# Low parts of the feed-forward weights: VectorE subtractions replaced by accumulating transfers issued from GpSimd

## The chip, the cores and the metric

The kernel runs on one core of one Trainium2 chip. The metric is the device time of one execution in microseconds, lower is better. The core has five engines that work side by side: TensorE (PE: matrix products into PSUM; PEld is its weight load), VectorE (DVE), ScalarE (ACT), GpSimd (POOL) and SyncE (SP), which here only issues transfers. Sixteen DMA engines move data between DRAM and on-chip memory (SBUF), whichever engine issued the transfer. An engine runs its instructions in the order of its queue.

## What is computed

One decoder block on 512 tokens of width 1024: a retention mixer and a short convolution run beside each other on the first normed input, are gated and merged, go through `mix_w_out`, and then a feed-forward layer of hidden width 2816 follows. The change touches only the weights from `mix_w_out` on:

```python
merged = jax.nn.sigmoid(g_a) * y_a + jax.nn.sigmoid(g_b) * y_b
x = x + gt_m[:, None, :] * (merged @ mix_w_out[l])

h = modulate(rmsnorm(x, norm_ffn_g[l]), sh_f, sc_f)
f = (jax.nn.silu(h @ ffn_w_gate[l]) * (h @ ffn_w_up[l])) @ ffn_w_down[l]
x = x + gt_f[:, None, :] * f
...
return rmsnorm(x, final_norm_g)
```

All is float32. `mix_w_out` is 1024x1024, `ffn_w_gate` and `ffn_w_up` are 1024x2816, `ffn_w_down` is 2816x1024.

## The kernel before

**Three products for one.** TensorE takes operands in float32r, a rounded form of float32. So each float32 operand is split in a high part (the value rounded to float32r) and a low part (what the rounding left), and a product is the sum of three: high by low, low by high, high by high. `mm3` (line 125) issues the three; the same order stands in `tm_gemm` (line 733).

**How a weight is split.** `split` (line 110) takes a view of a raw tile: ScalarE copies it into a tile of float32r (the high part, line 112), and VectorE subtracts that from the raw weights into a second tile (the low part, line 114). One such split covers 128x1024 elements, 512 KB, and is called a part below. High and low tiles come from the pool `wp` with four buffers each (tags "hi" and "lo"); raw tiles have three buffers. A tile is written again only when everything that read the former content of its buffer is done; the framework puts in the semaphores for this.

**Loads.** `load_raw` (line 103) issues one transfer from SyncE for a raw tile, mostly 1 MB, and keeps these loads in the order of the program.

**Feature-major products.** `proj` (line 537) loads a raw tile of 1024 rows by 256 columns, splits it in two parts of 128 columns ([128, 8, 128]: partition, k tile, column), and after each split issues 24 products of 128x128 by 128x512 into one PSUM bank (`fm_gemm`, line 530). In DRAM a row of such a part is 128 columns, 512 bytes. The feed-forward's gate and up matrices go through it under names that start with "f" ("fg" and "fu"), from the third chunk of 128 columns on: 10 calls for either matrix, so 20 calls and 40 parts. The first two chunks of either matrix are split elsewhere (in halves ahead of time for the gate, in `first_ffn`, line 829, with GpSimd subtracting for the up matrix).

**Token-major products.** `tm_gemm` (line 733) handles `mix_w_out` (name "mix", 4 parts for either half of the columns) and `ffn_w_down` (name "dn": 12 k tiles in a first round and 10 in a second, for two halves of the columns each, so 6+6+5+5 = 22 parts). A part is two k tiles by 512 columns ([128, 2, 512]); a row in DRAM is 2 KB. Again 24 products use one part. The first `early` k tiles are worked off for all four groups of tokens in turn, and then each group of tokens goes through the rest, so that the parts of the rest are held until the end of the half. For "mix", `early` is 4 in the first half and 0 in the second.

**Order.** The calls follow each other in the program: mix, then norm 2 by token tiles (`norm2`, whose `rest` trails behind the products of the second half of mix), then six pairs of chunks of gate and up with the down product of their twelve chunks, then five pairs with theirs, and the last norm. In that stretch GpSimd has only the two subtractions of `first_ffn`.

The line numbers of the profile are often those of the helper that records an operation (line 62 or 64), so groups are told apart by their tiles: `w_fg_l` is the low part of a gate weight, `w_fu_h` the high part of an up weight, `w_mix` and `w_dn` those of the two token-major matrices.

Of the kernel before, what the change touches and what calls it, by code (L numbers as in the profile page):

```python
# [19 lines left out]
P = 128  # L20
S = 512
# [26 lines left out]


class InTurn:  # L50
    """an engine that, while it is strict, keeps to the order of the program"""

    def __init__(self, tc, engine):
        self.tc, self.engine, self.strict, self.last = tc, engine, False, None
# [16 lines left out]
def block_kernel(ctx, tc, x, c, positions, ada_w, ada_b, norm_mix_g, w_in, conv_w, ret_w_out,  # L71
# [38 lines left out]
    def split(view, shape, name, eng=None):  # L110
# [3 lines left out]
        (eng or vec).tensor_tensor(lo, view, hi.bitcast(F32), ALU.subtract)  # L114
        return hi, lo

    def split_act(src, name, hi=None, lo=None, eng=None):
        hi = slot(name + "_h", F32R) if hi is None else hi
        lo = slot(name + "_l", F32R) if lo is None else lo
        act.copy(hi, src)  # L120
        (eng or vec).tensor_tensor(lo, src, hi.bitcast(F32), ALU.subtract)
        return hi, lo
# [3 lines left out]
        mm(o, lhsT=wh, rhs=xl, start=False, stop=False)  # L126
        mm(o, lhsT=wh, rhs=xh, start=False, stop=last)

# [1 line left out]
    small = nc.gpsimd  # L130
    rows = cp.tile([P, P], F32, name="rows")
    vec.memset(rows, 0.0)
# [45 lines left out]
        vecs.append(cp.tile([P, P], F32, name="vecs"))  # L178
        act.copy(vecs[0], tr[:, 0:P])

# [1 line left out]
    aw = ada_w[0].rearrange("(p k) n -> p k n", p=P)  # L182

    aw6 = ada_w[0].rearrange("(p k) (s n) -> p k s n", p=P, n=D)

    def ada_sum(pieces, n, name):
        """the product with cs, but for the sum over partitions"""
        a = sp.tile([P, n], F32, tag="adaacc", bufs=2, name=f"acc_{name}")
        for k, piece in enumerate(pieces):
            m = n // len(piece)  # L190
            for i, w in enumerate(piece):
                o = a[:, i * m:(i + 1) * m]
                if k == 0:
                    vec.tensor_scalar_mul(o, w, cs[:, 0:1])
                else:
                    vec.scalar_tensor_tensor(o, w, cs[:, k:k + 1], o, ALU.mult, ALU.add)
        return a
# [7 lines left out]
    ADA_PE = (0,)  # L205

    def ada_load(f, j, n):
        """pieces of the weights of shift and scale, for each k the columns of either"""
        s0 = 0 if f == "m" else 3
        cols = slice(j * P, (j + n) * P)  # L210
        pieces = []
        if f == "m":
            raw = wp.tile([P, KT, 2, P], F32, tag="raw", bufs=3, name=f"ada_{f}{j}")
            for k in range(0, KT, 4):
                for i in range(2):
                    load_raw.last = nc.sync.dma_start(raw[:, k:k + 4, i],
                                                      aw6[:, k:k + 4, s0 + i, cols])
            pieces = [[raw[:, k].rearrange("p s n -> p (s n)")] for k in range(KT)]
        else:
            for k in range(0, KT, 4):  # L220
                raw = wp.tile([P, 4, 2, n * P], F32, tag="raw", bufs=3, name=f"ada_{f}{j}_{k}")
                for i in range(2):
                    load_raw.last = nc.sync.dma_start(raw[:, :, i], aw6[:, k:k + 4, s0 + i, cols])
                pieces += [[raw[:, q].rearrange("p s n -> p (s n)")] for q in range(4)]
        ada_raw[f, j] = pieces

    def mod_vecs(f, j, n):
        """scale and shift of the k tiles j to j + n, by feature"""
        pieces = ada_raw.pop((f, j))
        pt = aux(f"mod_{f}{j}")  # L230
        if f == "m" and j in ADA_PE:
            for i in range(2):
                for k in range(KT):
                    mm(pt[:, i:i + 1], lhsT=pieces[k][0][:, i * P:(i + 1) * P], rhs=cs[:, k:k + 1],
                       start=k == 0, stop=k == KT - 1)
        else:
            a = ada_sum(pieces, 2 * n * P, f"{f}{j}")
            for i in range(2 * n):
                mm(pt[:, i:i + 1], lhsT=a[:, i * P:(i + 1) * P], rhs=ones32[:, 0:1],
                   start=True, stop=True)  # L240
        if not vecs:
            rows_by_feature()
        r0 = R_ADA + ADA["sc_" + f] // P + j
        r1 = R_ADA + ADA["sh_" + f] // P + j
        g0 = (R_GM if f == "m" else R_GF) + j
        av = mod["a_" + f][:, j:j + n]
        vec.tensor_tensor(av, pt[:, n:2 * n], vecs[0][:, r0:r0 + n], ALU.add)
        vec.scalar_tensor_tensor(av, av, 1.0, vecs[0][:, g0:g0 + n], ALU.add, ALU.mult)
        vec.tensor_tensor(mod["s_" + f][:, j:j + n], pt[:, 0:n], vecs[0][:, r1:r1 + n], ALU.add)

# [1 line left out]
    def half_ss(part, s, h, name):  # L252
        junk = sp.tile([P, S], BF16, tag="junk", bufs=2, name=f"{name}_j{h}")
        act.activation(junk[:, 0:part.shape[-1]], part, AF.Square, accum_out=s[:, h:h + 1])
# [5 lines left out]
        vec.reciprocal(r, r)  # L260
        return r

# [1 line left out]
    ang, angh, ah = misc("ang"), misc("angh", F32R), misc("ah")  # L264
    fr, fy, ft = misc("fr"), misc("fy"), misc("ft")
    ivp = inv_two_pi_parts()
    def to_frac(o, a, scale, n):
        """what is left of a * scale without its nearest integer"""
        pool.tensor_scalar(fy[:, 0:n], a, scale, MAGIC, ALU.mult, ALU.add)
        yield pool.tensor_scalar(fy[:, 0:n], fy[:, 0:n], 1.0, -MAGIC, ALU.mult, ALU.add)  # L270
        if scale != 1.0:
            pool.tensor_scalar(o, a, scale, 0.0, ALU.mult, ALU.add)
            a = o
        yield pool.tensor_tensor(o, a, fy[:, 0:n], ALU.subtract)
# [31 lines left out]
            if next(rotary_steps, None) is None:  # L306
                return

# [1 line left out]
    wi = w_in[0]  # L310
    xs = [[None] * 2 for _ in range(NT)]
    w_raw = {}
# [16 lines left out]
    for k in range(1, KT):  # L329
        loads.append(lambda k=k: ada_load("m", k, 1))  # L330
        if k % 2 == 0:
            loads.append(lambda k=k: w_load(k))
    # for each k: the loads made by then
    plan = [4, 6, 7, 9, 10, 12, 13, 13]
    pe.strict = pool.strict = True
    for fn in loads[:2]:
# [53 lines left out]
                             pool if (n, k) in W_POOL else None)  # L390

    def ready(k):
        """h of the k tile"""
        for fn in loads[made[0]:plan[k]]:
            fn()
        made[0] = max(made[0], plan[k])
        if k:
            mod_vecs("m", k, 1)
        if k == 0:
            for n in "vkq":  # L400
                w_split(n, k)
        tx = aux(f"tx_{k}")
        for t in range(NT):
            transpose(tx[:, t * P:(t + 1) * P],
                                xs[t][k // 4][:, (k % 4) * P:(k % 4 + 1) * P], ident)
        h32 = slot(f"h32_{k}")
        av, sv = mod["a_m"][:, k:k + 1], mod["s_m"][:, k:k + 1]
        act.activation(h32, tx, AF.Identity, scale=av, bias=sv)
        hist.append(act.copy(Hh[:, k, :], h32))
        hlast.append(vec.tensor_tensor(Hl[:, k, :], h32, Hh[:, k, :].bitcast(F32), ALU.subtract))  # L410
        if k % 2 and k + 1 < KT:
            for n in "vkq":
                w_split(n, k + 1)

    def products(k):
        """v by token, k and q by feature; what starts a bank clears the marks of all of it"""
        ops = []
        for part in range(3):
            at = k == 0 and part == 0, k == KT - 1 and part == 2
# [26 lines left out]
    rotary_on(100)  # L446
    pe.strict = pool.strict = False

    # ---- weights of the gate, of a pair of heads: first half of either head's features, then
    # the second ----  # L450
    gate_w = {}

    def gate_split(p, i):
# [10 lines left out]
        vec.tensor_scalar(fr, fr, HALF, -HALF, ALU.min, ALU.max)  # L464
    hist.append(act.last)

# [1 line left out]
    later = []  # L468

    def after(n, fn):  # L470
# [5 lines left out]
        for _, fn in due:  # L476
            fn()

# [1 line left out]
    ropeC = cp.tile([P, S], F32, name="ropeC")  # L480
    ropeS = cp.tile([P, S], F32, name="ropeS")

# [18 lines left out]
        return split_act(a, name)  # L501

    def value(pt, name, into, b):
        """v without its mean, of two token tiles of both heads"""
        pt = pt.rearrange("p (q n) -> p q n", n=P)
        mean = sp.tile([P, NT], F32, tag="vm", name=name + "_m")
        vec.tensor_reduce(mean, pt, axis=AX.X, op=ALU.add)
# [29 lines left out]
    def proj(src, col, Ah, Al, name, eng=None):  # L537
        raw = load_raw(src, 0, KT, col, 2 * P, "w_" + name)
        for i in range(2):
            wh, wl = split(raw[:, :, i * P:(i + 1) * P], [P, KT, P], f"w_{name}{i}", eng)  # L540
            yield i, fm_gemm(acc(f"p_{name}{i}"), wh, wl, Ah, Al)
            tick()

# [91 lines left out]
            gg[i] = slot(f"g{p}{i}")  # L635
            act.activation(gg[i], pt, AF.Silu)

# [1 line left out]
    conv_in = [None] * KT  # L639
    for p in range(KT // 2):  # L640
        cc, uu = {}, {}
# [16 lines left out]
            vec.tensor_tensor(uu[i], pt, uu[i], ALU.mult)  # L658
            conv_in[2 * p + i] = split_act(uu[i], f"ci{2 * p + i}")

# [1 line left out]
    def ret_out(p):  # L662
        raw = wp.tile([P, KT, 2 * P], F32, tag="raw", bufs=3, name=f"w_ya{p}")
        src = ret_w_out[0, :, 2 * p * P:2 * (p + 1) * P].rearrange(
# [64 lines left out]
        if p == 0:  # L729
            gate_vec("gt_m")  # L730

# [1 line left out]
    def tm_gemm(src, acts, k0, nk, h, groups, early, name, cut=False):  # L733
        """groups[t] = acts^T @ src[rows k0 on, half h]; cut: the last token tile by halves"""
        ws = []
        for kc in range(0, nk, 4):
            m = min(4, nk - kc)
            raw = load_raw(src, k0 + kc, m, h * S, S, f"w_{name}{h}_{kc}")
            for s in range(0, m, 2):
                ws.append(split(raw[:, s:s + 2, :], [P, 2, S], f"w_{name}{h}_{kc + s}"))  # L740

        parts = [(t, slice(0, S)) for t in range(NT)]
        if cut:
# [81 lines left out]
            if h == 1:  # L825
                norm2(t)

# [1 line left out]
    def first_ffn():  # L829
        """the first two chunks of either matrix, by halves of the tokens"""  # L830
        ws, pts = list(early_w), [acc(f"p_fg0{i}") for i in range(2)]
        raw = load_raw(ffn_w_up[0], 0, KT, 0, 2 * P, "w_fu0")
        for i in range(2):
# [76 lines left out]


def shape_constants():
    """Rotary frequencies and the decay of each head by distance: both follow from the shapes."""
    e = np.arange(0, P, 2, dtype=np.float32) / np.float32(P)
    inv_freq = np.float32(1) / np.power(10000.0, e.astype(np.float64)).astype(np.float32)
    lg = np.log(1.0 - 2.0 ** (-5.0 - np.arange(H))).astype(np.float32).astype(np.float64)
# [22 lines left out]
```

## Time and profile before

| | |
|---|---|
| median of 2 runs | 994.77 us (994.08 to 995.45) |
| span of the profiled execution, first to last instruction | 993.6 us |
| that execution has no time of its own beside its span; span against the median | 1.2 us less |
| bytes read from DRAM, written | 118.15 MB, 2.10 MB |
| transfers issued from GpSimd (software_dynamic) | 224 packets, 0.18 MB |

A row of the engine table gives busy time, share of the span and count. A row of a group gives the operation with what it writes and reads, its count, the total busy time, the mean of one in nanoseconds, and the idle time of its engine just before. A row of a window gives the busy time of each engine in that stretch, the clock granted to TensorE (1.00 is full), the busy share of the DMA engines and what they moved. That share is the summed time of packets over 16 engines, and since packets overlap in an engine it can exceed 1. The chain of waits follows the work that ended last back to the start.

### The profile page before, as it was taken

The page shows a single profiled execution, that of the slowest core. Times are in us where ns is not written, and L with a number is a line of the kernel's source. Part 1 is how long each engine was busy: PE and PEld are TensorE (multiplying, and loading weights), DVE is VectorE, ACT ScalarE, POOL GpSimd, SP SyncE. Part 2 cuts the span into 40 slices and gives each one's busy share as a digit, 9 for nine tenths or more (in the row PEclk, how much of TensorE's full clock was granted, in tenths as well). Part 3 has the DMA queues.
Part 4 walks back from the last instruction along what each step waited for, and adds up shares of the span by engine and source line. Part 5 has one row for each costly group of instructions (what it writes and reads, how often), then busy time and mean ns, then how long its engine had stood idle before and what let it go on. Part 6 is the DMA issues. An engine that isn't in the chain of part 4 may idle for free.

```text
span 993.6 us, 11278 instructions
## 1 busy us (share of the span) xinstructions
PE 959.1 (97%) x4579; PEld 809.2 (81%) x4579; DVE 566.9 (57%) x840; ACT 336.5 (34%) x496; POOL 55.4 (6%) x67
## 2 busy tenths in 40 slices
PE   5789999999999999999999999999999999999997
PEld 4677889898888888888888887988888888888886
DVE  5898767869575547455465456455633433433354
ACT  5225435444533323222223234432322112322223
POOL 4672000000000000000000001000000000000000
PEclk9899999999999999999999999999999999999999
DMA  9854221413222334676354351325622232242302
GB/s 270 235 156 141 96 96 43 144 48 98 83 93 78 128 85 140 185 197 220 128 170 155 124 188 43 107 85 170 211 85 85 91 121 85 85 137 75 106 1 85
DMA packets 116468, 120.98 MB, mean 122 GB/s; under 512 B 3444, under 2 KB 103840, under 8 KB 116416
## 3 DMA queue, kind: packets, MB, share of 16 engines
q1 hardware_dynamic: 116192, 120.08, 38.4%
q8 instruction: 36, 0.59, 0.2%
q0 software_dynamic: 224, 0.18, 0.1%
q14 instruction: 16, 0.13, 0.0%
HBM read 118.15 MB, written 2.10 MB: 121 GB/s over the span
## 4 chain that ended last, share of the span: by engine, by line
PE 89%; DVE 6%; ACT 1%; DMA 1%; SPq 1%; issue 1%; DVEq 0%; ACTq 0%
PE p_fu L64 12%; PE p_fg L64 12%; PE dn L64 12%; PE p_ga L64 4%; PE p_gb L64 4%; PE p_u L64 4%; PE p_b L64 4%; PE p_c L64 4%; PE p_yb L64 4%; PE p_ya L64 4%; PE mix L64 4%; PE p_k L64 3%; PE p_q L64 3%; PE p_g L64 3%; PE p_v L64 3%; DVE acc_m L64 2%
## 5 line engine op out<-in xcount | busy, mean ns | idle before, releaser
L64 PE MATMUL p_fu<-Gl,w_fu_h 128*128 128x512 f32 (+1 forms) x192 | 71.4, 372 | 0.0
L64 PE MATMUL p_fu<-Gh,w_fu_l 128*128 128x512 f32 (+1 forms) x192 | 71.3, 372 | 0.0
L64 PE MATMUL p_fu<-Gh,w_fu_h 128*128 128x512 f32 (+1 forms) x192 | 71.3, 371 | 0.0
L64 PE MATMUL dn<-w_dn_h,fa_l 128*128 128x512 f32 (+1 forms) x176 | 67.5, 384 | 0.0
L64 PE MATMUL dn<-w_dn_l,fa_h 128*128 128x512 f32 (+1 forms) x176 | 67.5, 383 | 0.0
L64 PE MATMUL dn<-w_dn_h,fa_h 128*128 128x512 f32 (+1 forms) x176 | 67.4, 383 | 0.0
L64 PE MATMUL p_fg<-Gh,w_fg_l 128*128 128x512 f32 x160 | 62.3, 389 | 0.0
L64 PE MATMUL p_fg<-Gl,w_fg_h 128*128 128x512 f32 x160 | 62.3, 389 | 0.0
L64 PE MATMUL p_fg<-Gh,w_fg_h 128*128 128x512 f32 x160 | 62.3, 389 | 0.0
L64 DVE TENSOR_TENSOR w_dn_l<-w_dn,w_dn_h 128x1024 fp32r<-128x1024 f32 x22 | 26.9, 1225 | 57.5 <-ACT w_dn_h L64 57.5
L64 DVE TENSOR_TENSOR w_fg_l<-w_fg,w_fg_h 128x1024 fp32r<-128x1024 f32 x20 | 24.5, 1224 | 56.5 <-ACT w_fg_h L64 56.5
L64 ACT CAST w_fu_h<-w_fu 128x1024 fp32r<-128x1024 f32 x22 | 23.2, 1053 | 73.8 <-PE p_fu L64 40.9
L64 ACT CAST w_dn_h<-w_dn 128x1024 fp32r<-128x1024 f32 x22 | 23.1, 1049 | 65.6 <-PE dn L64 39.4
L64 DVE TENSOR_TENSOR fg<-p_fu,fg 128x512 f32<-128x512 f32 x22 | 15.2, 691 | 50.8 <-PE p_fu L64 50.7
L64 PEld LDWEIGHTS p_fu<-Gh,w_fu_h 128*128 128x128 f32 x192 | 36.2, 188 | 6.2
L64 PEld LDWEIGHTS p_fu<-Gl,w_fu_h 128*128 128x128 f32 x192 | 36.2, 188 | 6.2
L64 PEld LDWEIGHTS p_fu<-Gh,w_fu_l 128*128 128x128 f32 x192 | 36.2, 188 | 6.1
L64 ACT ACTIVATE fg<-p_fg 128x512 f32<-128x512 f32 x22 | 13.2, 598 | 80.1 <-PE p_fg L64 80.1
L64 PEld LDWEIGHTS dn<-w_dn_h,fa_l 128*128 128x128 f32 x176 | 33.1, 188 | 6.6
L64 PEld LDWEIGHTS dn<-w_dn_l,fa_h 128*128 128x128 f32 x176 | 33.1, 188 | 6.5
L64 PEld LDWEIGHTS dn<-w_dn_h,fa_h 128*128 128x128 f32 x176 | 33.1, 188 | 6.5
L64 PEld LDWEIGHTS p_fg<-Gh,w_fg_h 128*128 128x128 f32 x160 | 30.0, 188 | 6.3
(339 smaller groups left out, 2565.9 us busy)
## 6 DMA issues: line engine op xcount, KB each, us to landing
w_fg<-in_ffn_w_gate_dram SPq DMA_DIRECT2D x11, 1024.0 KB, 5.2
w_fu<-in_ffn_w_up_dram SPq DMA_DIRECT2D x11, 1024.0 KB, 5.2
w_dn<-in_ffn_w_down_dram SPq DMA_DIRECT2D x10, 1024.0 KB, 4.9
ada_m<-in_ada_w_dram SPq DMA_DIRECT2D x32, 256.0 KB, 6.1
ada_f<-in_ada_w_dram SPq DMA_DIRECT2D x16, 512.0 KB, 4.7
x<-in_x_dram SPq DMA_DIRECT2D x16, 256.0 KB, 6.1
w_g<-in_w_in_dram SPq DMA_DIRECT2D x4, 1024.0 KB, 5.0
w_c<-in_w_in_dram SPq DMA_DIRECT2D x4, 1024.0 KB, 5.0
```

Of the source, the lines that this page charges most:

```text
L64: self.last = op(*args, **kw)
```

## The change

A second splitting function, `split_dma`, is used for the parts of `proj` whose name starts with "f" (40 parts) and for all of `tm_gemm` (8 + 22 parts). It makes the high part as before. Then ScalarE writes the negated weights into the low tile, rounded to float32r as the high part is, and a transfer issued from GpSimd adds the float32 weights from DRAM to what stands in the low tile. The transfer reads the same weights in DRAM that `load_raw` brought, a second time, in rows of 512 bytes (`proj`) or 2 KB (`tm_gemm`). VectorE's subtraction falls away for these 70 parts. The rest of the diff takes comments out.

```diff
+    def split_dma(view, shape, name, src):
+
+        hi = wp.tile(shape, F32R, tag="hi", name=name + "_h")
+        act.copy(hi, view)
+        lo = wp.tile(shape, F32R, tag="lo", name=name + "_l")
+        act.mul(lo, view, -1.0)
+        nc.gpsimd.dma_start(lo, src, accum_op=ALU.add)
+        return hi, lo
...
     def proj(src, col, Ah, Al, name, eng=None):
         raw = load_raw(src, 0, KT, col, 2 * P, "w_" + name)
         for i in range(2):
-            wh, wl = split(raw[:, :, i * P:(i + 1) * P], [P, KT, P], f"w_{name}{i}", eng)
+            part = src[:, col + i * P:col + (i + 1) * P].rearrange("(k p) n -> p k n", p=P)
+            if name[0] == "f":
+                wh, wl = split_dma(raw[:, :, i * P:(i + 1) * P], [P, KT, P], f"w_{name}{i}", part)
+            else:
+                wh, wl = split(raw[:, :, i * P:(i + 1) * P], [P, KT, P], f"w_{name}{i}", eng)
             yield i, fm_gemm(acc(f"p_{name}{i}"), wh, wl, Ah, Al)
             tick()
...
     def tm_gemm(src, acts, k0, nk, h, groups, early, name, cut=False):
...
             raw = load_raw(src, k0 + kc, m, h * S, S, f"w_{name}{h}_{kc}")
             for s in range(0, m, 2):
-                ws.append(split(raw[:, s:s + 2, :], [P, 2, S], f"w_{name}{h}_{kc + s}"))
+                part = src[(k0 + kc + s) * P:(k0 + kc + s + 2) * P, h * S:(h + 1) * S].rearrange(
+                    "(k p) n -> p k n", p=P)
+                ws.append(split_dma(raw[:, s:s + 2, :], [P, 2, S], f"w_{name}{h}_{kc + s}", part))
```

## The prediction, made before the result was seen

> **What bounds the kernel now.** I read the engine table first, then the chain of waits, then the busy time by stage.
>
> ```profile
> span 993.6 us, 11278 instructions
> PE 959.1 (97%) x4579; PEld 809.2 (81%) x4579; DVE 566.9 (57%) x840; ACT 336.5 (34%) x496; POOL 55.4 (6%) x67
> PE 89%; DVE 6%; ACT 1%; DMA 1%; SPq 1%; issue 1%; DVEq 0%; ACTq 0%
> 573.00 32.64 PE mix L64 x144
> 844.61 10.88 PE p_fg L64 x48
> ```
>
> TensorE is busy for 97% of the span and holds 89% of the chain. A product takes 32.64 / 144 = 0.227 us, and the 24 products of a weight part 10.88 / 2 = 5.44 us: the pace at which low parts must be ready.
>
> ```profile
> core 0: us, PE busy (x) PEld busy (x) DVE busy (x) ACT busy (x) POOL busy (x), PEclk, DMA share, GB/s
> 614.00:636.00 22.00, 19.55 (x133) 18.31 (x132) 16.53 (x29) 13.29 (x27) 4.87 (x2) 0.92 0.36 120
> 647.60:757.60 110.00, 110.00 (x490) 91.12 (x489) 54.34 (x81) 32.50 (x44) 0.00 (x0) 1.00 0.41 134
> 757.60:822.90 65.30, 65.30 (x289) 54.07 (x288) 24.47 (x28) 13.18 (x14) 0.00 (x0) 1.00 0.30 97
> 822.90:931.70 108.80, 108.80 (x481) 90.12 (x480) 38.21 (x42) 30.53 (x39) 0.00 (x0) 1.00 0.30 97
> 931.70:982.40 50.70, 50.70 (x236) 42.34 (x235) 23.29 (x33) 15.30 (x25) 0.00 (x0) 1.00 0.12 42
> ```
>
> In the gate and up stages (647.6 to 757.6, 822.9 to 931.7) and the down stages between and behind them TensorE never pauses at full clock; VectorE, ScalarE and the DMA engines all have room. Only around norm 2 (614 to 636) is TensorE idle, for 22.00 - 19.55 = 2.45 us. So relief of VectorE is worth almost nothing, and the question is whether the new way delivers a part every 5.44 us.
>
> **What is removed.**
>
> ```profile
> L64 DVE TENSOR_TENSOR w_mix_l<-w_mix,w_mix_h x8: 1214/1226/1226, 558.3 to 596.3; 128x1024 fp32r<-128x1024 f32 x8
> L64 DVE TENSOR_TENSOR w_dn_l<-w_dn,w_dn_h 128x1024 fp32r<-128x1024 f32 x22 | 26.9, 1225 | 57.5 <-ACT w_dn_h L64 57.5
> L64 DVE TENSOR_TENSOR w_fg_l<-w_fg,w_fg_h 128x1024 fp32r<-128x1024 f32 x20 | 24.5, 1224 | 56.5 <-ACT w_fg_h L64 56.5
> L64 DVE TENSOR_TENSOR w_fu_l<-w_fu,w_fu_h x20: 1214/1226/1226, 645.9 to 911.1; 128x1024 fp32r<-128x1024 f32 x20
> L64 ACT CAST w_fu_h<-w_fu 128x1024 fp32r<-128x1024 f32 x22 | 23.2, 1053 | 73.8 <-PE p_fu L64 40.9
> ```
>
> 70 subtractions of 1.225 us, 85.8 us of VectorE. All but those near norm 2 lie beside a busy TensorE, so they free nothing on the path. Bounds of the gain: 0 and the 2.45 us; I take 0, because ScalarE gets more work at the same place.
>
> **What ScalarE gains.** 70 negations of the size of the cast, 1.05 us each, 73.5 us. In the stage 822.9 to 931.7 ScalarE goes from 30.5 to 30.5 + 20 x 1.05 = 51.5 us of 108.8: hidden by TensorE; without that cover it would cost the 1.05 us per part. It lengthens the way of a part, though. Queued behind a negation are the silu and the casts of the next chunk, whose consumers are several parts away. Near norm 2 two negations (2.1 us) go into ScalarE's queue among the steps of norm 2 while VectorE loses two subtractions there; bounds -2.45 and +2.1, taken as +1.
>
> **How much time a part has.**
>
> ```profile
> 828.82 1.04 ACT L64 CAST w_fg_h<-w_fg 128x1024 fp32r<-128x1024 f32 x1
> 829.89 1.23 DVE L64 TENSOR_TENSOR w_fg_l<-w_fg,w_fg_h 128x1024 fp32r<-128x1024 f32 x1 [3.72 <-ACT w_fg_h L64]
> w_dn<-in_ffn_w_down_dram SPq DMA_DIRECT2D x10, 1024.0 KB, 4.9
> w_dn<-in_ffn_w_down_dram SPq DMA_DIRECT2D x2, 512.0 KB, 3.2
> ```
>
> The cast of 828.82 is for the products of 844.61, and it ends at 829.86. After the negation 844.61 - 829.86 - 1.05 = 13.7 us remain for issue and landing. A plain load of 512 KB lands in 3.2 us, so one accumulate alone, even three times as long, is late for nothing in a steady stage. What decides is the rate.
>
> **What POOL gains.** 70 transfers in an otherwise empty queue, each waiting there for its negation.
>
> ```profile
> L135 POOL DMA_DIRECT2D rows<-in_norm_mix_g_dram x1 | 0.6, 563 | 0.0
> L154 POOL DMA_DIRECT2D ivf<-in_inv_freq_dram x1 | 0.6, 577 | 0.0
> q0 software_dynamic: 224, 0.18, 0.1%
> q1 hardware_dynamic: 116192, 120.08, 38.4%
> ```
>
> Issuing 8 rows took 0.56 us, 128 rows 0.58: hardly any cost per row. A gate or up part has 128 x 8 = 1,024 rows of 512 bytes. Low end 0.58 us; high end, if all of the 0.58 were per row, 8 x 0.58 = 4.6 us, and 9.2 if source and destination are written separately. I take under 2 us, since 8 and 128 rows cost the same; then POOL keeps pace. SP's queue gets no step more; its loads only share the DMA engines.
>
> **What the DMA engines gain, the term that decides.** The trace of before has no accumulating transfer, so its price is bounded by plain packets. The busiest stretches hold mostly the modulation's 512-byte rows:
>
> ```profile
> 16.00:20.00 4.00, 1.38 (x4) 0.69 (x4) 3.74 (x13) 3.13 (x7) 1.13 (x1) 1.00 1.20 298
> 20.00:24.00 4.00, 3.67 (x12) 3.10 (x12) 3.86 (x7) 3.04 (x6) 1.79 (x3) 1.00 1.21 297
> 28.00:32.00 4.00, 4.00 (x13) 3.23 (x13) 3.17 (x5) 2.77 (x5) 2.71 (x2) 1.00 1.22 290
> ```
>
> There the engines reach a share of 1.22, which I take as full. One engine moved 290 / 1.22 / 16 = 14.9 to 298 / 1.20 / 16 = 15.5 GB/s per unit of share, so 512 bytes cost about 33 ns. In the down stage (2 KB rows) it is 97 / 0.30 / 16 = 20.2, so 2 KB cost 101 ns.
>
> An accumulate reads the source, reads the destination and writes it. A plain packet already pays for one read and one write. Low end: the add is free and a piece costs one plain packet (33 ns). Middle: two packets, one for each read (66). Upper middle: three, the write-back hidden by nothing (99). High end: two packets at the price of the GpSimd queue's own, 0.001 x 993.6 x 16 / 224 = 71 ns, so 142. The 71 has a wide rounding (0.1% may be 0.05 or 0.15). I take 99, which lies between what the two rows give for two reads.
>
> By stage, with 1,024 / 16 = 64 pieces per engine and part: a gate or up part costs 64 x 0.099 = 6.3 us of share. Stage 822.9 to 931.7: 20 parts give 126.7, the loads of now 0.30 x 108.8 = 32.6; together 159.3, over 1.22 = 130.6 us against 108.8: +21.8. Stage 647.6 to 757.6: 126.7 + 0.41 x 110 = 171.8, over 1.22 = 140.8: +30.8. Down stages: a part has 16 pieces of 2 KB per engine, 16 x 3 x 0.101 = 4.85 us; 12 x 4.85 + 19.6 = 77.8, over 1.22 = 63.8 of 65.3; 10 x 4.85 + 6.1 = 54.6, over 1.22 = 44.8 of 50.7: both hidden.
>
> **Where a part has no slack.**
>
> ```profile
> 593.49 1.05 ACT L64 CAST w_mix_h<-w_mix 128x1024 fp32r<-128x1024 f32 x1 [1.95 <-issue]
> 595.06 1.04 ACT L64 CAST w_mix_h<-w_mix 128x1024 fp32r<-128x1024 f32 x1
> 964.58 1.05 ACT L64 CAST w_dn_h<-w_dn 128x1024 fp32r<-128x1024 f32 x1 [0.95 <-PE dn_last L64]
> 970.10 12.28 PE dn L64 x54
> ```
>
> The second half of mix starts after 96 products, at 573.0 + 96 x 0.227 = 594.8, and goes through all four of its parts for the first tokens: it needs the third at 597.5 and the fourth at 598.8. Their buffers come free so late that the casts start at 593.49 and 595.06. With the negations in line the fourth is ready to issue at about 597.7, and with 0.6 for the issue and 3.2 (a plain 512 KB load) lands at 601.5, with three passes and the third beside it at about 605: a stall of 2.7 to 6.5; I take 6, nearer the three passes of the sum. The last part of the second down stage has its cast at 964.58 and is needed soon after 970.10, at about 972.5; landing about 972 to 974: taken as +1.
>
> Sum: 21.8 + 30.8 + 6 + 1 + 1 = +60.6 us on a span of 993.6 and, by the 1.2 us between span and median, 994.8 + 60.6 = 1055 us.
>
> **Rivals.** (B) The DMA engines keep up: two packets for a piece. Then a part costs 4.2 us, the stages need (84.5 + 32.6) / 1.22 = 96 of 108.8 us and (84.5 + 45.1) / 1.22 = 106 of 110, and only the places without slack are left, +8: 1003 us, no change that can be measured. It decides at the price of a piece: at 70 ns in the first of these stages, (1.22 x 110 - 45.1) / (20 x 64), and at 78 in the second. For it speaks that the packets overlap so well in the early stretches; against it, that the GpSimd queue's own packets were priced at 71, more than twice 33.
>
> The Trainium skill, "Collectives: The Full Stack", section "The bandwidth ceiling: the fold count and why AG ≠ RS ≠ AR", says that an add inside a DMA engine costs no time for the adding and halves the rate, because two sources are read. By that rule the piece costs two packets and the time is the 1003 of this rival; no trace here shows an accumulate, and the rule's transfers were long, so it does not lift this rival over the forecast.
>
> (C) The transfers don't overlap, or POOL's writing of them is the bound. Written separately for source and destination at 9.2 us a part, 40 parts cost 40 x (9.2 - 5.44) = 150 us: 1155 with the rest. One after another, with 1.5 us of fixed landing (3.2 less the 4.9 - 3.2 that another 512 KB adds), 3 x 64 x 0.033 / 1.22 = 5.2 for the passes, 0.6 for the issue and 1.3 for the raw load's share, a part takes 8.6 us, 40 x 3.2 = +128, and the down parts about 7.4, 22 x 2 = +44: 1180 with mix. Against it speak the equal issue times of 8 and 128 rows and the early overlap.
>
> The Trainium skill, "DMA: Bandwidth & Descriptors", section "SWDGE vs HWDGE vs iDMA", says that for transfers issued from GpSimd a small core computes each descriptor in software. That speaks for the first half of this rival; the two issue rows above don't show a cost per row.
>
> (D) Norm 2 gains from the freed VectorE: at most 2.45 us, 992. It would not count as faster.
>
> **How the numbers follow.** About 2%, some 20 us, is what a measurement can tell from no change. Forecast (a piece between 75 and 145 ns, 1015 to 1150 us): 0.47. B (997 to 1014): 0.36. C (1150 and over): 0.15. D: 0.02. Slower is forecast and C, 0.62; same is B and nearly all of D, 0.37; faster 0.01. The range goes from B's low end (2.7 us of stall, 997) to C's 1180 and leaves out about 0.1 at either end; the likeliest case alone is 1015 to 1150.
>
> **What would show it.** In the changed profile: no `w_fg_l`, `w_fu_l` rows of VectorE, 70 negations on ScalarE near 1.05 us, 70 transfers on POOL. If I am right, the DMA share in the gate and up stages stands near 1.2, TensorE there waits for the low parts' transfers, and the stages last near 141 and 131 us while the down stages keep their length. If B holds, the share is near 1 and they keep 110 and 109. If C holds, TensorE waits with the share well under 1, and either POOL is busy all through or the landing times are long. A down stage that grows as much as the gate stages would refute the price by rows, and a mix without a stall the count of its slack.

## The result, and the profile after

The changed kernel takes 1004.17 us (median of two runs, 1003.67 to 1004.68) against 994.77: a ratio of 1.0096, 95% interval 1.0077 to 1.0115. It is 9.4 us slower: the interval leaves out 1, so the loss is real, but it is under half of the 20 us that the prediction called no change, and 51 us under the predicted 1055. The profiled span is 1002.9 us against 993.6.

First the engine table, the DMA queues and the chain's shares of the changed kernel, read as before.

```profile
span 1002.9 us, 11461 instructions
PE 960.7 (96%) x4579; PEld 809.6 (81%) x4579; DVE 482.7 (48%) x770; ACT 401.8 (40%) x566; POOL 154.0 (15%) x137
q1 hardware_dynamic: 116192, 120.08, 39.3%
q0 software_dynamic: 49984, 36.88, 25.9%
PE 81%; DVE 5%; issue 5%; DMA 4%; POOL 2%; ACT 1%; SPq 1%; POOLq 0%; ACTq 0%; DVEq 0%
```

TensorE works almost as long as before (960.7 to 959.1), so the 9.3 us more in the span are mostly waits, and some slow clock. VectorE lost 84.2 us, ScalarE gained 65.3 and GpSimd's engine 98.6 us of issuing. The GpSimd queue moves 36.7 MB more. The chain now has 4% DMA in it.

The stages of the changed kernel, with the columns of the prediction's table (clock, DMA share and GB/s at the end):

```profile
617.20:639.20 22.00, 20.70 (x148) 18.84 (x147) 15.87 (x36) 17.72 (x36) 8.29 (x4) 1.00 0.64 150
650.80:767.00 116.20, 111.72 (x489) 92.24 (x489) 31.32 (x61) 51.26 (x65) 29.98 (x20) 0.99 1.13 220
767.00:832.30 65.30, 65.30 (x290) 54.10 (x289) 11.07 (x16) 23.53 (x25) 13.98 (x12) 1.00 0.89 187
832.40:941.10 108.70, 108.70 (x481) 90.04 (x480) 13.84 (x20) 50.11 (x61) 31.30 (x21) 1.00 1.10 197
941.10:991.70 50.60, 50.60 (x237) 42.34 (x236) 15.00 (x26) 21.41 (x32) 8.39 (x7) 1.00 0.60 117
```

The first row answers to norm 2 (614 to 636 before). Three of the four stages below it have the length of before to within 0.1 us, with TensorE busy all through. Only the first gate and up stage grew, and its DMA share (1.13) is hardly higher than that of the second (1.10), which lost nothing.

Where the delay arises shows in the chain in order of time (start, length, what): before, then after.

```profile
636.10 5.76 PE p_fg L64 x48
757.57 65.28 PE dn L64 x288
822.85 10.88 PE p_fg L64 x48
931.65 29.24 PE dn L64 x129
```

```profile
639.28 5.76 PE p_fg L64 x48
767.08 65.28 PE dn L64 x288
832.36 10.88 PE p_fg L64 x48
941.16 29.59 PE dn L64 x132
```

The changed kernel is 3.2 us late at the second half of the first chunks, 9.5 us late at the down product, and stays 9.5 us late to the end. So 3.2 us come from mix and norm 2, 6.3 us from the first gate and up stage, and nothing from anywhere else.

TensorE's waits from mix on in the changed kernel (what waited, for what, total us, times, longest us); in the kernel before, the only one in that stretch was `tx` for `xn`, 2.4 us, and it has gone:

```profile
PE p_fg L64 <- DMA w_fg_l<-in_ffn_w_gate_dram: 4.5, 1, 4.5
PE mix L64 <- DMA w_mix_l<-in_mix_w_out_dram: 4.0, 1, 4.0
PE p_fg L64 <- ACT Gh L64: 0.7, 1, 0.7
PE p_fg L64 <- DVE Gl L64: 0.6, 1, 0.6
```

70 accumulating transfers, and TensorE waits for two of them.

**The first wait, in mix.** The third part of the second half: its issue, TensorE's row at its arrival, and a window behind it.

```profile
594.46 1.20 POOL L123 DMA_DIRECT2D w_mix_l<-in_mix_w_out_dram  x1 [8.32 <-PE mix L64]
594.46 7.36 DMA w_mix_l<-in_mix_w_out_dram
601.86 0.80 PE L64 MATMUL mix<-w_mix_l,mg_h 128*128 128x512 f32 x1 [4.04 <-DMA w_mix_l<-in_mix_w_out_dram]
602.00:606.00 4.00, 4.00 (x12) 3.15 (x13) 0.00 (x0) 0.00 (x0) 0.00 (x0) 0.62 1.12 278
```

The part is issued at 594.46, as soon as its buffer and negation allow, lands 7.36 us later, and TensorE has stood for 4.04 us. Then the granted clock is 0.62 for 4 us: 12 products instead of 4 / 0.227 = 17.6, another 1.3 us. Of these 5.3 us, 2.1 are made up at norm 2, where the 2.4 us wait for `xn` is gone, 0.7 + 0.6 stand in its place, and the clock is 1.00 instead of 0.92; 3.2 stay.

**The second wait, in the first gate and up stage.** The release is followed back here in the order of time: VectorE, ScalarE, POOL, the transfer, TensorE.

```profile
704.64 0.35 DVE L64 TENSOR_SCALAR acc_gt_f<-ada_gt_f,cs 128x256 f32<-128x256 f32 x1 [10.56 <-DMA ada_gt_f<-in_ada_w_dram]
706.48 0.68 DVE L64 TENSOR_TENSOR fg<-p_fu,fg 128x512 f32<-128x512 f32 x1
707.20 0.63 ACT L64 CAST fa_h<-fg 128x512 fp32r<-128x512 f32 x1 [11.27 <-DVE fg L64]
707.72 1.06 ACT L64 ACTIVATE w_fg_l<-w_fg 128x1024 fp32r<-128x1024 f32 x1
709.13 1.55 POOL L123 DMA_DIRECT2D w_fg_l<-in_ffn_w_gate_dram  x1 [12.24 <-ACT w_fg_l L64]
709.13 11.93 DMA w_fg_l<-in_ffn_w_gate_dram
721.10 0.79 PE L64 MATMUL p_fg<-Gh,w_fg_l 128*128 128x512 f32 x1 [4.48 <-DMA w_fg_l<-in_ffn_w_gate_dram]
721.10 12.79 PE p_fg L64 x48
```

`ada_gt_f` is weights of the modulation that SyncE loads in this stage and VectorE multiplies in small steps between its other work. The load is late; VectorE stands 10.56 us at its head, with `fg` (gate times up) queued behind it. ScalarE stands 11.27 us at the cast of that `fg`, with the negation of the next gate part queued behind it. So that part's transfer is issued at 709.13, needs 11.93 us, and TensorE stands 4.48 us; the next 48 products take 12.79 instead of 10.88 us at a lower clock. Together 6.4 us, the 6.3 that the chain gave.

The load is late for two reasons. The first is that it lands more slowly, as the DMA engines are shared. The issue rows, with KB each and the median us to landing, before and then after; the rows below them, on issuing and negating, are read in the last sections:

```profile
ada_gt_f<-in_ada_w_dram SPq DMA_DIRECT2D x4, 1024.0 KB, 6.6
```

```profile
ada_gt_f<-in_ada_w_dram SPq DMA_DIRECT2D x4, 1024.0 KB, 9.5
w_fg_l<-in_ffn_w_gate_dram POOLq DMA_DIRECT2D x20, 512.0 KB, 9.6
w_dn_l<-in_ffn_w_down_dram POOLq DMA_DIRECT2D x22, 512.0 KB, 6.4
L123 POOL DMA_DIRECT2D w_fu_l<-in_ffn_w_up_dram x20 | 31.1, 1554 | 91.4 <-ACT w_fu_l L64 76.3
L123 POOL DMA_DIRECT2D w_dn_l<-in_ffn_w_down_dram x22 | 26.3, 1195 | 93.4 <-ACT w_dn_l L64 76.7
L64 ACT ACTIVATE w_dn_l<-w_dn 128x1024 fp32r<-128x1024 f32 x22 | 23.3, 1060 | 64.7 <-PE dn L64 39.0
```

The second is that it is issued later. The load in question is the third of the four; its issue and VectorE's first use of it before, then its issue after:

```profile
685.66 0.55 SPq L701 DMA_DIRECT2D ada_gt_f<-in_ada_w_dram  x1
693.49 0.35 DVE L64 TENSOR_SCALAR acc_gt_f<-ada_gt_f,cs 128x256 f32<-128x256 f32 x1 [1.59 <-DMA ada_gt_f<-in_ada_w_dram]
```

```profile
692.59 1.53 SPq L714 DMA_DIRECT2D ada_gt_f<-in_ada_w_dram  x1
```

From issue to use it took 7.8 us before and 12.0 after (704.64 - 692.59). The issue itself is 6.9 us later, 3.7 more than the 3.2 us by which the whole kernel is late there. Just ahead of it in SyncE's queue stands a load of `w_fg` that needs the buffer of the second `ada_gt_f`: it waited 7.6 us for that to land and 4.0 us for VectorE to sum it. So one slow landing delays the next load.

### The profile page after: what moved, and what is told of

Same layout as the page of the kernel before. It is cut to its first block, busy times and chain, and to the rows that moved or that the text cites. A ratio compares the mean times of both kernels' runs of the same rounds, so it can differ in the third digit from the quotient of the medians.

```text
span 1002.9 us, 11461 instructions
## 1 busy us (share of the span) xinstructions
PE 960.7 (96%) x4579; PEld 809.6 (81%) x4579; DVE 482.7 (48%) x770; ACT 401.8 (40%) x566; POOL 154.0 (15%) x137
## 4 chain that ended last, share of the span: by engine, by line
PE 81%; DVE 5%; issue 5%; DMA 4%; POOL 2%; ACT 1%; SPq 1%; POOLq 0%; ACTq 0%; DVEq 0%
PE dn L64 11%; PE p_fg L64 9%; PE p_fu L64 8%; PE p_ga L64 4%; PE p_gb L64 4%; PE p_u L64 4%; PE p_c L64 4%; PE p_yb L64 4%; PE p_b L64 4%; PE p_ya L64 4%; PE mix L64 4%; PE p_k L64 3%; PE p_q L64 3%; PE p_g L64 3%; PE p_v L64 3%
## 5 line engine op out<-in xcount | busy, mean ns | idle before, releaser
L123 POOL DMA_DIRECT2D w_mix_l<-in_mix_w_out_dram x8 | 9.7, 1213 | 506.4 <-ACT sgb L64 478.2
L64 DVE TENSOR_TENSOR dx_gt_f<-dn,gt_f 128x512 f32<-128x512 f32 (+1 forms) x16 | 10.8, 673 | 81.1 <-PE dn L64 81.1
L64 ACT ACTIVATE w_dn_l<-w_dn 128x1024 fp32r<-128x1024 f32 x22 | 23.3, 1060 | 64.7 <-PE dn L64 39.0
L123 POOL DMA_DIRECT2D w_fu_l<-in_ffn_w_up_dram x20 | 31.1, 1554 | 91.4 <-ACT w_fu_l L64 76.3
L123 POOL DMA_DIRECT2D w_fg_l<-in_ffn_w_gate_dram x20 | 31.1, 1554 | 77.7 <-ACT w_fg_l L64 72.5
L64 ACT ACTIVATE w_fu_l<-w_fu 128x1024 fp32r<-128x1024 f32 x20 | 21.2, 1061 | 48.6 <-PE p_fu L64 40.7
L123 POOL DMA_DIRECT2D w_dn_l<-in_ffn_w_down_dram x22 | 26.3, 1195 | 93.4 <-ACT w_dn_l L64 76.7
L64 PEld LDWEIGHTS p_fg<-Gh,w_fg_l 128*128 128x128 f32 x160 | 30.4, 190 | 11.0 <-DMA w_fg_l<-in_ffn_w_gate_dram 4.7
```

Of the source, the lines that this page charges most:

```text
L64: self.last = op(*args, **kw)
L123: nc.gpsimd.dma_start(lo, src, accum_op=ALU.add)
```

## The experiments

All kernels are the changed one with the edit shown; the ratio is to the kernel before, run on the same chip. Theories: **L** (latency): the loss is the two waits, each for a part whose way from raw tile to low tile has become too long for its place, the second through the late `ada_gt_f`. **R** (rate): the transfers fill the DMA engines, and the loss is their load.

| kernel | accumulates | us | ratio (95%) |
|---|---|---|---|
| after | 70 | 1004.17 | 1.0096 (1.0077 to 1.0115) |
| mix_sub | 62 | 999.84 | 1.0057 (1.0040 to 1.0073) |
| gtf_late | 70 | 1004.82 | 1.0109 (1.0094 to 1.0124) |
| both_undone | 62 | 999.38 | 1.0050 (1.0028 to 1.0073) |
| no_add | 30 (40 copies) | 997.95 (one run) | before there 994.52 |
| gtf_nodep | 70 | 998.83 | 1.0043 (1.0030 to 1.0057) |
| rows_256 | 110 (80 of half size) | 1009.11 | 1.0138 (1.0101 to 1.0176) |
| second_round | 42 | 994.67 | 0.9999 (0.9986 to 1.0011) |
| extra_load | 70 | 1063.17 | 1.0693 (1.0671 to 1.0714) |
| mix_sub_nodep | 62 | 994.09 | 0.9998 (0.9988 to 1.0008) |
| only_fu0 | 2 | 992.89, repeat 992.05 | 0.9980 (0.9966 to 0.9994), 0.9980 (0.9971 to 0.9989) |
| fu0_dve | 0 | 990.90 | 0.9965 (0.9953 to 0.9978) |
| fu0_one | 1 | 989.97 | 0.9959 (0.9946 to 0.9971) |

**mix_sub: mix split by VectorE again.**

```diff
-                ws.append(split_dma(raw[:, s:s + 2, :], [P, 2, S], f"w_{name}{h}_{kc + s}", part))
+                if name == "mix":
+                    ws.append(split(raw[:, s:s + 2, :], [P, 2, S], f"w_{name}{h}_{kc + s}"))
+                else:
+                    ws.append(split_dma(raw[:, s:s + 2, :], [P, 2, S], f"w_{name}{h}_{kc + s}", part))
```

> Only the eight parts of mix go back to VectorE's subtraction; gate, up and down keep the accumulates. Theory (two separate waits): the wait for w_mix_l (4.0 us in the changed kernel, and about 1.3 us of lowered clock behind it) goes, the wait for w_fg_l near 721 us (4.5 us and about 1.9 us of lowered clock) stays: 1004.2 - 5.3 = about 999 us. Rival (the DMA engines' rate sets the end, and the mix wait is only where it shows first): the time is made up later, 1002 to 1004 us, with a longer wait for w_fg_l.

The wait in mix is gone, the old one at norm 2 is back at 2.4 us, and a wait for `w_fg_l` of 2.9 us stays. The time falls from 1004.17 to 999.84, as theory L said (about 999): mix costs about 4 us by this edit (3.9 by the ratios, which are less disturbed by the change of chip).

**gtf_late: VectorE's work on `ada_gt_f` moved two steps behind its load.** Shown is the end of the edit; `loaded` issues the load, `summed` has VectorE's work, and `lag` is 2 for `gt_f`.

```diff
+            if lag:
+                after(2 * j + 1, lambda j=j: loaded(j))
+                after(2 * j + 1 + lag, lambda j=j: summed(j))
```

> All accumulates stay. The four loads of ada_gt_f are issued where they were, but VectorE sums them two chunks of 24 products later, so that a late landing holds nothing in VectorE's queue; the same bytes move in the same stage. Theory (the second wait comes from the order of the queues: late ada_gt_f holds VectorE, VectorE's product fg holds ScalarE's cast, and the negation of w_fg stands behind that): the wait for w_fg_l goes, 1004.2 - 6.3 = about 998 us. Rival (in that stage the DMA engines are simply full, share 1.14): the wait stays, 1002 to 1005 us.

The edit didn't do what it was made for: VectorE still stood 11.3 us at the longest for `ada_gt_f`, and TensorE 4.0 us for `w_fg_l`. The time is that of the changed kernel. It tells nothing of the theory, since the cause was not removed.

**both_undone: the two edits together.**

> Both edits together: mix subtracted on VectorE, ada_gt_f summed later, 62 accumulates left. Theory: both waits gone, 1004.2 - 11.6 = about 993 us, level with the kernel before or up to 2 us under it, since norm 2 lasted some 2 us less in the changed kernel. Rival (the DMA engines' rate costs time by itself): 997 to 1003 us, with TensorE waiting somewhere in the gate and up stages.

The six runs scatter from 995.78 to 1003.54. The trace is of the slowest of them: there a wait of 5.6 us for `w_fg_l` stays, and VectorE still stands 12.5 us for `ada_gt_f`. The median missed the expected 993. For the same reason as gtf_late it decides nothing beyond mix.

**no_add: the 40 gate and up transfers without the add** (the low part is then the weight itself).

```diff
-        nc.gpsimd.dma_start(lo, src, accum_op=ALU.add)
+        if name.startswith("w_f"):
+            nc.gpsimd.dma_start(lo, src)
+        else:
+            nc.gpsimd.dma_start(lo, src, accum_op=ALU.add)
```

> The transfers of the gate and up parts copy the weights over the negated high part instead of adding to it, so the low parts there hold the weights themselves and the output differs; mix and down add as before. Theory (an adding piece costs two plain packets, because it reads twice): a piece falls from 68 to about 34 ns, and the DMA share of the second gate and up stage from 1.10 to about 0.70. Rival (a packet issued from GpSimd costs twice one issued from SyncE, added or not): the share stays near 1.1. The time is between 994 and 1003 us by either; the share decides.

The wait for `w_fg_l` is gone, and the part lands in 5.1 us instead of 9.6. One window in the second stage:

```profile
837.00:937.00 100.00, 100.00 (x442) 82.79 (x442) 13.55 (x20) 46.59 (x57) 17.90 (x19) 1.00 0.83 190
```

With 0.30 for the loads of before and 100 / 5.44 = 18.4 parts, a part costs (0.83 - 0.30) x 100 / 18.4 = 2.9 us of share, 45 ns for each of its 64 pieces per engine. With the add it is (1.10 - 0.30) x 108.8 / 20 = 4.35 us, 68 ns. So a piece with the add costs 1.5 times such a copy, and about two of the 33 ns packets. Neither expectation held: the share is 0.83, between 0.70 and 1.1.

These prices take the other loads at their share of before. A second count, from the GpSimd queue's own share, needs no such term. mix_sub_nodep (below) has 20 gate and up parts more than second_round, and its queue takes 23.9% of 990.8 us against 15.4% of 992.8, 83.9 us more: 65.5 ns a piece. no_add's queue takes 21.4% of 996.2 us, 46.6 us less than the changed kernel's, so the add costs 18 ns and the copy 47. By this count the factor is 1.4.

**gtf_nodep: VectorE multiplies a table that lies in SBUF instead of `ada_gt_f`, which is still loaded.**

```diff
-            a = ada_sum([[raw[:, k]] for k in range(KT)], 2 * P, f"{name}{j}")
+            src = [[raw[:, k]] for k in range(KT)]
+            if name == "gt_f":
+                src = [[ropeC[:, 0:2 * P]] for k in range(KT)]
+            a = ada_sum(src, 2 * P, f"{name}{j}")
```

> All accumulates stay, and the four loads of ada_gt_f still move their 4 MB in the same stage, but VectorE's sums for gt_f read a rotary table that is resident instead of them, so the gate vector gt_f and the output differ. Nothing in VectorE's queue waits for those loads any more. In the run gtf_late this wait had only moved (VectorE still waited 11.3 us for ada_gt_f). Theory (the second wait comes through VectorE's and ScalarE's queues): no wait for w_fg_l, 1004.2 - 6.3 = about 998 us, with the DMA share of the stage as before (1.1). Rival (the DMA engines are full there): the wait stays, 1003 to 1005 us.

This takes away VectorE's wait, and with it the time that a landed `ada_gt_f` keeps its buffer for VectorE; all transfers stay, and the `ada_gt_f` loads even take 13.2 us (median). The time falls to 998.83, the ratio by 0.0053, 5.3 us. The same stretch of the first stage, and the only late part left:

```profile
640.00:757.60 117.60, 117.60 (x568) 99.36 (x567) 21.06 (x37) 54.88 (x69) 31.02 (x21) 1.00 1.10 212
```

```profile
PE mix L64 <- DMA w_mix_l<-in_mix_w_out_dram: 4.6, 1, 4.6
```

TensorE doesn't pause at a share of 1.10. The late load did harm only through VectorE's standing at it; that is L. The rival, full DMA engines, foresaw 1003 to 1005 us.

**rows_256: each gate or up transfer in two, with rows of 256 bytes.** Shown is what names that start with `w_f` get instead of the one transfer.

```diff
+            for c in range(2):
+                cs = slice(c * 64, c * 64 + 64)
+                nc.gpsimd.dma_start(lo[:, :, cs], src[:, :, cs], accum_op=ALU.add)
```

> Each accumulate of a gate or up part is cut in two transfers of 64 columns, so its pieces in DRAM are 256 bytes, 128 per engine and part instead of 64. If a piece's cost is mostly fixed (some 50 to 68 ns whatever its length), a part costs 6.4 to 8.7 us of share, the stages exceed 1.2 and become bound by the DMA engines: the second gate and up stage lasts 132 to 170 us instead of 108.8, the whole 1050 to 1130 us. If the cost goes by bytes, a part stays at 4.3 us, and the time within 1000 to 1010 us. POOL issues 2 x about 1.5 us for a part, under the 5.44 us of its products, by either.

```profile
835.00:935.00 100.00, 100.00 (x442) 82.60 (x441) 13.14 (x19) 46.66 (x56) 57.63 (x37) 1.00 1.43 195
```

A part now costs (1.43 - 0.30) x 100 / 18.4 = 6.1 us of share, 48 ns for each of 128 pieces and about as much as the 6.3 that the prediction gave a part. Yet at a share of 1.43 TensorE is busy for 100.00 of 100 us at full clock, where the author's expectation for such a price was a stage of 132 to 170 us. So the share of 1.22 was no limit, and a share close to the predicted one did not slow this stage. The bytes per us are those of before the edit (195 GB/s against 197), so it says nothing of a limit in bytes. The kernel is 4.9 us slower than the changed one through the known place: behind the same late `ada_gt_f` the part now lands in 17.9 us instead of 11.9, and the waits for `w_fg_l` are 7.1 us, with 1.6 more for `w_fg_h`.

**second_round: accumulates only in the second gate and up stage and in the down products (42 of 70).**

```diff
-            if name[0] == "f":
+            if name[0] == "f" and int(name[2:]) >= 1536:
```

(with mix as in mix_sub)

> Accumulates only where the changed kernel showed no wait: all of the down matrix and the gate and up parts of the second round (42 parts); mix and the first round's gate and up go back to VectorE. Theory (a stage at share 1.10 costs TensorE nothing as long as parts have slack): level with the kernel before, 993 to 996 us. Rival (the accumulates cost a little everywhere, by the DMA engines or by ScalarE): 42/70 of the 9.4 us, about 1000 us.

The share in that stage is 1.08, TensorE is busy for 100.00 of 100 us there, no wait for a low part is left, and the ratio is 0.9999 (0.9986 to 1.0011). These 42 transfers cost nothing that is measured.

**extra_load: more plain loads beside the accumulates of the second stage, to find the real limit.**

```diff
+        if name[0] == "f" and int(name[2:]) >= 1536:
+            for j in range(4):
+                with tc.issue_after(load_raw.last.ins):
+                    load_raw.last = nc.sync.dma_start(
                        scr(f"more_{name}{j}", F32, [P, 2, 2 * P]),
                        src[2 * j * P:2 * (j + 1) * P, col:col + 2 * P].rearrange(
                            "(k p) n -> p k n", p=P))
```

> The changed kernel with 1 MB of further loads (four transfers of 256 KB in rows of 1 KB, read by nobody) behind each weight load of the second round's gate and up parts: 96 GB/s more on 194. Theory (a share above 1 is overlap of packets and not a limit; rows_256 ran at 1.43 without a wait): the share rises to about 1.4 or above, that stage stays at 108.8 us, 1003 to 1006 us. Rival (the engines are full in bytes near 200 GB/s of accumulates and loads, and rows_256 moved no more bytes): low parts land late, the stage grows by 10 to 35 us, 1013 to 1040 us.

Inconclusive. The extra loads waited for their scratch buffers at the head of SyncE's queue (58.5 us in three waits for `fa_l`), and so delayed the weight loads behind them. The share in the slowed stretches was 0.88 to 1.00, below that of the changed kernel, so the 59 us over the changed kernel can't be read as a limit of rate. At which load the engines are really full stays open; a version with buffers of its own wasn't tried.

**mix_sub_nodep: mix_sub and gtf_nodep together, 62 of the 70 accumulates left.**

> mix_sub and gtf_nodep together: mix subtracted on VectorE, 62 accumulates in gate, up and down, and the sums for gt_f read a resident table instead of the loaded ada_gt_f, so that gate vector and the output differ. Theory (the two waits are the whole of the loss, and nothing of it is the DMA engines' rate): 999.8 - 994.5 = 5.3 and 998.8 - 994.6 = 4.2 us each left by one edit, so the other's share goes too: level with the kernel before, 993.5 to 996 us. Rival (a third cost hides behind the two, or the waits feed each other): 997 to 999 us.

```profile
645.00:755.00 110.00, 110.00 (x490) 91.13 (x490) 20.39 (x36) 51.23 (x64) 30.08 (x20) 1.00 1.19 233
755.00:820.30 65.30, 65.30 (x290) 54.09 (x289) 11.07 (x16) 23.54 (x25) 14.04 (x12) 1.00 0.88 187
820.30:929.10 108.80, 108.80 (x482) 90.12 (x481) 13.83 (x20) 50.26 (x61) 31.38 (x21) 1.00 1.10 197
```

Both waits are gone, the stages have the length of before at shares up to 1.19, and the ratio is 0.9998 (0.9988 to 1.0008). So the two waits are the whole loss within what is measured, about 1 us. The traffic has its part in them, as it makes landings longer (`ada_gt_f` 6.6 to 9.5 us), but no stage is bound by its amount, which is what R said.

**only_fu0, fu0_dve, fu0_one: the gap at norm 2.** All 70 parts are split by VectorE again; changed is only who makes the two low parts of `w_fu0`, GpSimd's subtractions in both kernels: two accumulates (only_fu0), two VectorE subtractions (fu0_dve), one of either (fu0_one).

```diff
-            ws.append(split(raw[:, :, i * P:(i + 1) * P], [P, KT, P], f"w_fu0{i}", pool))
+            ws.append(split(raw[:, :, i * P:(i + 1) * P], [P, KT, P], f"w_fu0{i}"))
```

(shown for fu0_dve)

> The kernel before, but for the first two up parts, whose low part GpSimd subtracted (2.4 us each, beside norm 2 on VectorE): these two are made by negation and accumulate. Theory: in the kernel before VectorE's steps of norm 2 stretch while GpSimd subtracts (two Gl subtractions 2.44 us instead of 1.29, a 128x1 sum 2.31 instead of 0.15), so without it TensorE's wait there (2.4 us) shrinks: 992 to 994 us. Rival (ScalarE's two negations of 1.06 us go into the same chain and take the place of the wait): 994 to 996 us.

> The kernel of only_fu0 again, beside the two that follow, to settle by how much it is under the kernel before: 0.997 to 0.999 of it, 992 to 994 us.

> No accumulate anywhere: the kernel before, but the two subtractions that GpSimd made beside norm 2 go to VectorE (1.22 us each). Theory A (the gain of only_fu0 comes from taking GpSimd off SBUF while VectorE works, and VectorE's own 2.4 us more stand in the same chain): level with the kernel before, 993.5 to 996 us, worse than only_fu0. Theory B (the gain is only GpSimd's absence, VectorE has room): 991 to 993 us, as good as only_fu0, and the accumulate is not needed.

> The first of the two up parts by negation and accumulate, the second by VectorE's subtraction. In only_fu0 TensorE waited 2.5 us for the second part's transfer, which landed 10.4 us after its issue; that wait goes, and VectorE gets 1.2 us in norm 2's chain. Theory (the transfer's landing is what is left): 990.5 to 992.5 us. Rival (the subtraction in the chain costs what the landing gives): 992.5 to 994.5 us.

Two of VectorE's rows at norm 2, first in the kernel before, then in fu0_dve:

```profile
616.62 2.44 DVE L64 TENSOR_TENSOR Gl<-h,Gh 128x512 fp32r<-128x512 f32 x2 [1.44 <-ACT Gh L64]
618.99 2.31 DVE L64 TENSOR_TENSOR n_r<-n2s 128x1 f32<-128x1 f32 x1
```

```profile
615.34 1.29 DVE L64 TENSOR_TENSOR Gl<-h,Gh 128x512 fp32r<-128x512 f32 x2
616.55 0.15 DVE L64 TENSOR_TENSOR n_r<-n2s 128x1 f32<-128x1 f32 x1
614.00:640.00 26.00, 26.00 (x203) 24.92 (x202) 14.93 (x29) 14.64 (x30) 0.00 (x0) 1.00 0.32 102
```

In the kernel before, GpSimd's two subtractions stand at 615.51 (2.40 us) and 618.81 (2.48). Beside them VectorE needs 2.44 us for two subtractions that else take 1.29, and 2.31 for 0.15. In only_fu0, where GpSimd doesn't subtract either and VectorE gets no more work, the two rows are 1.29 and 0.15 as well, so it is GpSimd's work that stretches them. With the subtractions on VectorE TensorE is busy for all 26 us from 614 to 640. fu0_dve and fu0_one are the fastest kernels of the study, 0.35% and 0.41% under the kernel before; their intervals overlap, so which is better is not settled. The gain needs no accumulate. only_fu0 gains less: TensorE waits there for a low part that a transfer brings (2.5 us, 2.9 in the repeat), which fu0_one avoids with one accumulate.

## Why the prediction was wrong in its size

Its range (997 to 1180) holds the measured 1004.17; its forecast of 1055 and the forecast's own range from 1015 don't. It gave slower 0.62 and no change 0.37, and by its own line of 20 us no change it was. Step by step:

- **Removed subtractions, worth 0: right** for the stages. VectorE's 84 us freed no time.
- **Negations on ScalarE, hidden: right in size** (1.06 us each; 50.1 of 108.7 us in the second stage, predicted 51.5). Their place in the queue was examined only for what stands behind a negation. What stands ahead of one was not asked for: that is where the second wait comes from.
- **POOL under 2 us for each issue: right**, 1.55 us for 1,024 rows and 1.20 for 256. Rows do cost something (0.35 us between the two), and POOL is far from a bound, at 31.3 of 108.7 us.
- **Price of a piece, 99 ns: the step that failed.** Measured are 68 ns (65.5 by the second count), and (0.89 - 0.30) x 65.3 / 12 / 16 = 200 ns for 2 KB, twice 101. That is the price of two packets, the bound that rival B took. With 68 ns the prediction's own sum gives (87.0 + 32.6) / 1.22 = 98 of 108.8 us and (87.0 + 45.1) / 1.22 = 108 of 110: the +21.8 and +30.8 us are gone, and nothing but the places without slack is left. The rule cited from the Trainium skill ("Collectives: The Full Stack", "The bandwidth ceiling: the fold count and why AG ≠ RS ≠ AR") gives twice a plain packet, and against the loads from SyncE the trace agrees (68 to 33); against a converting copy on the same queue it measured 1.4 to 1.5 (68 to 45).
- **"A share of 1.22, which I take as full": wrong as well.** The price became time only through this limit. rows_256 puts nearly the forecast's load per part on the engines and runs at 1.43 without a pause (the forecast's 159.3 us are 1.46 of 108.8). The busiest stretch seen was taken for a limit, while the share adds up packets that overlap. Rival B's threshold of 70 to 78 ns rested on the same limit, and falls with it. Where the true limit lies is open.
- **"one accumulate alone, even three times as long, is late for nothing in a steady stage": wrong in the first stage.** The 13.7 us were counted from a cast that is on time. When VectorE and ScalarE stand for 11 us at a late load, the part starts late and 11.93 us of landing don't fit: 6.3 us, a term that the sum doesn't have. gtf_nodep removes just this wait and gains 5.3 us.
- **Mix, +6: mechanism and size right, the part wrong.** The third part stalled TensorE, not the fourth: 4.0 us, and 1.3 at the lower clock, a cost that the prediction didn't count. Landing was 7.4 us, near the 6.7 that it took (598.3 to 605).
- **Norm 2, +1: wrong in sign.** 2.1 us of the delay were made up there. **Last down part, +1:** no wait; the delay is 9.5 us at 941 and 9.3 in the span.

Rival B named 1003 us, 1.2 us from the measured time, but its sum was mix 6, norm 2 1 and the last part 1: it is right that no stage is bound by rate, and it lacks the late load, which makes up most of the loss. That its number is so near is luck. C falls by the shares above 1 with a busy TensorE. D is refuted as a gain of the whole, though the gap it speaks of could be closed by other means (fu0_dve).

## What to carry to other kernels

The DMA share of the profile was no gauge of how full the engines are: look whether anything waits at such a share before dividing by it. When an engine's work is replaced by a transfer, follow the whole way of the slowest piece through every in-order queue, and ask for what stands ahead of it there, above all loads that the new traffic makes later. And price not only the wait of TensorE but the slow clock behind it: here 4.0 and 4.5 us of standing cost 5.3 and 6.4.

## What the runs showed of the hardware

- The summed packet time of the DMA engines reached 1.43 over 100 us with TensorE busy all through (rows_256), where the busiest stretches of the kernel before show 1.22.
- An accumulate of float32 into float32r through the GpSimd queue took 48 ns of an engine's share for 256 bytes, 68 for 512 and 200 for 2 KB; the converting copy without the add 45 for 512 (a second count gives 65.5 and 47 for the two at 512).
- After TensorE had stood for 4.04 us the granted clock was 0.62 over the next 4 us (602 to 606), and after 4.48 us 0.52 over 3 us (721 to 724).
- Two VectorE subtractions with both operands in SBUF took 2.44 us together instead of 1.29 beside a GpSimd subtraction, and a step on 128x1 elements 2.31 instead of 0.15 (before against fu0_dve and only_fu0). The Trainium skill ("SBUF — State Buffer", "Who interferes with whom") says that a VectorE instruction with two SBUF inputs contends with a GpSimd instruction that reads SBUF; the trace agrees.
